# Last eight block halves in banks of their own, and a last norm with ScalarE's root

## The chip, the cores and the metric

One core of one Trainium2 chip runs the whole program. The metric is the device time of one execution in microseconds; less is better. The engines are TensorE (PE: matmuls, with their weight loads as PEld), VectorE (DVE), ScalarE (ACT), GpSimd (POOL) and SyncE (SP), which here only issues DMAs.

## The reference, cut to what matters

The program is one inference step of a hybrid decoder layer over 512 prompt positions and 8 sample tokens, with D = 1024. Only its end matters here: the down projection of the gated MLP, the residual add and the final norm.

```python
def rmsnorm(x, g):
    xf = x.astype(jnp.float32)
    y = xf * lax.rsqrt(jnp.mean(xf * xf, axis=-1, keepdims=True) + EPS)
    return y.astype(x.dtype) * g

# conv_ffn:       (jax.nn.silu(gate) * val) @ w_down      D_FF = 2816
# decoder_layer:  return h + y_ffn
# reference:      y_prompt = rmsnorm(hp, g_final); y_sample = rmsnorm(hs, g_final)
```

## The kernel before

Activations are kept transposed: `hT` is the residual as [128 channels, 8 blocks of channels, 2 halves of tokens, 260 tokens], so block d holds channels 128d to 128d+127, and a half holds 256 prompt positions and 4 sample tokens. A product in full precision is made of three reduced ones: the weight and the activation are each split in a high and a low part (`w_hi`, `w_lo`, `h_hi`, `h_lo`), and hi*hi, hi*lo and lo*hi are summed in PSUM. ScalarE makes the high parts, VectorE the low parts.

The down projection runs over three parts of the 22 hidden tiles (8, 8 and 6). The first two parts, and blocks 0 to 3 of the third, handle both halves of the tokens with one split weight (lines 1533 to 1553). The last four blocks of the third part (`D0` = 4 to 7) are done half by half (lines 1589 to 1617): first all four blocks for the first half, then, with the weights split once in `wl_hi` and `wl_lo`, all four for the second. Each of these eight block halves is 6 tiles times 3 products = 18 matmuls of 260 columns into PSUM; then VectorE adds the result to `hT` (line 1605, which the profile lists as the helper's line 120), ScalarE squares it (`sq`, line 1607), GpSimd adds the square to `acc4` (line 1609), and `final_block` lets ScalarE write `hT` times `g_final` to `hg`. PSUM has three tiles "pp" of two banks each and two tiles "t" of one bank. Here blocks 4 and 5 of a half share one "pp" tile, `ps[:, 0]` and `ps[:, 1]`, and so do blocks 6 and 7.

`half_norm` sums the squares over channels with matmuls against a column of ones (line 1567): 128, 128 and 4 tokens, one column of PSUM each. On the second half the last square isn't added by GpSimd but summed by a second set of those matmuls. VectorE scales the sums, adds eps and forms the reciprocal root by an integer first guess and three Newton steps (`rsqrt`, lines 216 to 228, 12 small operations). Two transposes and a small matmul spread the result over the partitions (lines 1577 and 1578), and ScalarE copies it to `R`. `half_store` then multiplies `hg` by `R` in three pieces of 3, 3 and 2 blocks, on VectorE, GpSimd and VectorE, and issues a store of each from SP, ScalarE and SP.

The order of the instructions on each engine is made by the framework's scheduler from the order of the program and the readiness of operands; `tc.high_priority()` moves the last norm up. A matmul that starts in a tile waits until the readers of the tile's former content are done. `half_norm(0)` and `half_store(0)` are called through the list `todo`, after block 4 of the second half.

Of the kernel before, what the change touches and what calls it, by code (L numbers as in the profile page):

```python
# [12 lines left out]
AF = mybir.ActivationFunctionType  # L13
OP = mybir.AluOpType
AX = mybir.AxisListType

P = 128
D = 1024
KT = D // P
SEQ = 512  # L20
NB = 8
HT = 260
# [12 lines left out]
EPS = 1e-6  # L35
# [66 lines left out]
def run(gen):  # L102
    for _ in gen:
        pass
# [3 lines left out]
def decoder_step(ctx: ExitStack, tc: tile.TileContext, A, O):  # L108
    nc = tc.nc
    dve, act, pe, pool, sp = nc.vector, nc.scalar, nc.tensor, nc.gpsimd, nc.sync  # L110
# [5 lines left out]
    def acopy(o, i, scale=1.0):  # L116
        act.activation(o, i, AF.Copy, scale=scale)  # L117

    def tt(o, a, b, op, eng=None):
        (eng or dve).tensor_tensor(o, a, b, op=op)  # L120
# [10 lines left out]
    def open_pool(name, side="left", psum=False):  # L131
        es = ExitStack()
        kw = {"space": bass.MemoryType.PSUM} if psum else {}
        p = es.enter_context(tc.tile_pool(name=name, bufs=1, reuse_waits="tile", side=side, **kw))
        return p, es

    def ptile(pool_, shape, tag, dt=F32, bufs=1, name=None):
        return pool_.tile(shape, dt, tag=tag, name=name or tag, bufs=bufs)
# [7 lines left out]
    rp, _e = open_pool("rp")  # L146
# [4 lines left out]
    ident = cst[:, C_ID:C_ID + 128]  # L151
    px0, es_px0 = open_pool("px0")
    hT = ptile(px0, [P, KT, 2, HT], "x0")
# [17 lines left out]
    ones = const.tile([P, 2], F32, name="ones")  # L171
# [4 lines left out]
    def load_w(src, kt=KT, name="w_raw"):  # L176

        t = ptile(wp, [P, KT, 256], "w_raw", bufs=2, name=name)
        sp.dma_start(t[:, :kt, :], src.rearrange("(k p) c -> p k c", p=P))
        return t  # L180
# [35 lines left out]
    def rsqrt(ms, n):  # L216
        i = ptile(rp, [P, 8], "rs_i", I32, bufs=2)[:, :n]
        y = ptile(rp, [P, 8], "rs_y", bufs=2)[:, :n]
        t = ptile(rp, [P, 8], "rs_t", bufs=2)[:, :n]
        hx = ptile(rp, [P, 8], "rs_hx", bufs=2)[:, :n]  # L220
        dve.tensor_scalar(i, ms.bitcast(I32), 1, None, op0=OP.logical_shift_right)
        dve.tensor_scalar(y.bitcast(I32), i, -1.0, float(0x5F3759DF), op0=OP.mult, op1=OP.add)
        dve.tensor_scalar(hx, ms, -0.5, None, op0=OP.mult)
        for _ in range(3):
            tt(t, y, y, OP.mult)
            tt(t, t, hx, OP.mult)
            dve.scalar_tensor_tensor(y, t, 1.5, y, op0=OP.add, op1=OP.mult)
        return y
# [59 lines left out]
    def bank(tag):  # L288
        p, n = ps_pool[tag]
        return ptile(p, [P, 2, 512] if tag.startswith("pp") else [P, 512], tag, bufs=n, name="ps_" + tag)  # L290
# [3 lines left out]
    def pp():  # L294
        return bank("pp")
# [901 lines left out]
    hT = ptile(hp, [P, KT, 2, HT], "hT")  # L1197
# [40 lines left out]
    for q in range(2):  # L1238
        raw = ptile(wp, [P, 4, 512], "w_raw", bufs=2, name="w_oa")
# [6 lines left out]
        for l in range(4):  # L1246
            d = 4 * q + l
            w = split_w(raw[:, :, l * P:(l + 1) * P], 4)
            ps = pp()
# [35 lines left out]
    raw = load_w(A["w_xq"][0][:, 0:256])  # L1285
# [133 lines left out]
    ff, _e = open_pool("ff")  # L1419
# [22 lines left out]
    for q in range(4):  # L1442
        raw = load_w(A["w_xo"][0][:, q * 256:(q + 1) * 256]) if q else None
        for l in range(2):
            d = 2 * q + l
            if q == 0:
                ps = ps_xo[l]
                project(ps, w_xo[l], xs_o, ks=range(6, KT))
            else:
                w = split_w(raw[:, :, l * P:(l + 1) * P])  # L1450
                ps = pp()
# [17 lines left out]
    w_down = A["w_down"][0]  # L1469
# [54 lines left out]
    parts = ((0, 8), (8, 16), (16, 22))  # L1524
# [3 lines left out]
    def final_block(d, hf=(0, 1)):  # L1528

        for r in hf:  # L1530
            acopy(hg[:, r, d], hT[:, d, r], scale=vec[:, 68 + d:69 + d])

    for pi, (j0, j1) in enumerate(parts):
# [5 lines left out]
        kt = j1 - j0  # L1539
        for q in range(4 if pi < 2 else 2):  # L1540
            raw = load_w(w_down[j0 * P:j1 * P, q * 256:(q + 1) * 256], kt)
            for l in range(2):
                d = 2 * q + l
                w = split_w(raw[:, :kt, l * P:(l + 1) * P], kt)
                ps = bank("pp")
                project(ps, w, lambda k: hid[j0 + k], 0, kt)
                tt(hT[:, d], hT[:, d], ps[:, :, :HT], OP.add)
                if pi == 2:
# [6 lines left out]
    D0 = 4  # L1555
    kt = parts[2][1] - parts[2][0]
    wl_hi, wl_lo = (ptile(ab3, [P, KT, 2, HT], t, F32R, name="wl").rearrange("p a r t -> p (a r t)")
                    [:, 0:(KT - D0) * kt * P].rearrange("p (d k c) -> p d k c", k=kt, c=P) for t in ("x3_hi", "x3_lo"))

    def half_norm(hf, *rest):  # L1560

        ps = bank("t")
        squares = (acc4[:, hf],) + rest
        for j, a in enumerate(squares):
            for i in range(3):
                n = P if i < 2 else 4
                pe.matmul(ps[0:n, i:i + 1], a[:, i * P:i * P + n], ones[:, 0:1], start=(j == 0 and i == 0),
                          stop=(j == len(squares) - 1), skip_group_check=True)
        ms = ptile(rp, [P, 8], "ss", bufs=2, name="ms")
        dve.memset(ms, 1.0)  # L1570
        with (tc.high_priority() if hf else ExitStack()):
            dve.tensor_scalar(ms[:, 0:2], ps[:, 0:2], 1.0 / D, EPS, op0=OP.mult, op1=OP.add)
            dve.tensor_scalar(ms[0:4, 2:3], ps[0:4, 2:3], 1.0 / D, EPS, op0=OP.mult, op1=OP.add)
            rs = rsqrt(ms[:, 0:3], 3)
            ps = bank("t")
            for i in range(2):
                pe.transpose(ps[:, i * P:(i + 1) * P], rs[:, i:i + 1].to_broadcast([P, P]), ident)
            pe.matmul(ps[:, 256:260], rs[0:4, 2:3].to_broadcast([4, P]), ident[0:4, 0:4], start=True, stop=True)
            R = ptile(rp, [P, 2, HT], "R", bufs=2, name="R4")[:, 0]
            acopy(R, ps[:, 0:HT])  # L1580
        return R

    def half_store(hf, R):
        for d0, d1, eng, q in ((0, 3, dve, sp), (5, 8, pool, act), (3, 5, dve, sp)):
            o = hg[:, hf, d0:d1]
            tt(o, o, R[:, None, :].to_broadcast([P, d1 - d0, HT]), OP.mult, eng)
            q.dma_start(O["y_t"][:, hf, d0:d1], o)

    todo = [lambda: final_block(D0 - 1)]
    for hf in range(2):  # L1590
        for d in range(D0, KT):
            dl, l = d - D0, d % 2
            if l == 0:
                ps = bank("pp")
                if hf == 0:
                    raw = load_w(w_down[parts[2][0] * P:, d * P:(d + 2) * P], kt)
            if hf == 0:
                with ExitStack():
                    acopy(wl_hi[:, dl], raw[:, :kt, l * P:(l + 1) * P])
                tt(wl_lo[:, dl], raw[:, :kt, l * P:(l + 1) * P], wl_hi[:, dl].bitcast(F32), OP.subtract)  # L1600
            for k in range(kt):
                xhi, xlo = hid[parts[2][0] + k]
                for j, (a, x) in enumerate(((wl_hi, xhi), (wl_hi, xlo), (wl_lo, xhi))):
                    pe.matmul(ps[:, l, :HT], a[:, dl, k, :], x[:, hf, :], start=(k + j == 0), stop=(k == kt - 1 and j == 2))  # L1604
            tt(hT[:, d, hf], hT[:, d, hf], ps[:, l, :HT], OP.add)
            sq = ptile(ff, [P, SEQ + NB], "sg", bufs=2, name="sqh")[:, 0:HT]
            act.activation(sq, hT[:, d, hf], AF.Square)
            if hf == 0 or d < KT - 1:
                pool.tensor_tensor(acc4[:, hf], acc4[:, hf], sq, op=OP.add)
            while todo:  # L1610
                todo.pop(0)()
            todo.append(lambda d=d, hf=hf: final_block(d, (hf,)))
        if hf == 0:
            todo.append(lambda: half_store(0, half_norm(0)))
    while todo:
        todo.pop(0)()
    half_store(1, half_norm(1, sq))


_OUTS = [("y_t", (P, 2, KT, HT)), ("kv_t", (6, P, 2, HT)), ("win_keep", (NB, WIN - 1, 2, 2, 64)),  # L1620
# [74 lines left out]
```

## Time and profile before

| | us |
|---|---|
| median of 3 runs | 899.33 (898.23 to 901.22) |
| the profiled execution, device time | 901.21 |
| its span, first to last instruction | 899.1 |
| TensorE matmuls busy | 857.2 (95%) |
| TensorE weight loads busy | 789.3 (88%) |
| VectorE, ScalarE, GpSimd busy | 567.5, 369.6, 121.6 |

Times in the rows are microseconds from the start of the span. Matmuls are pipelined: one of 260 columns shows about 0.28 us, and the next starts about 0.12 us after it. A row "x2" merges neighbours, and its time is that from the first start to the last end. In square brackets stands the idle time of the engine before the instruction, and what ended it. The granted clock of TensorE is 1.00 at 2.4 GHz and 0.50 at 1.2 GHz. VectorE's, ScalarE's and GpSimd's helper operations are listed under the helper's line (L120, L117).

### The profile page before, as it was taken

The numbers are of one execution on the slowest core, as the hardware profiler recorded it, in microseconds if no ns is written. First come the engines' busy times: TensorE is split into PE (matmuls) and PEld (weight loads), VectorE is DVE, ScalarE is ACT, GpSimd is POOL, SyncE is SP. The second block draws the span as 40 slices with busy tenths as digits, with TensorE's granted clock in tenths as the row PEclk, the third lists the DMA queues.
The fourth block names the chain that finished last, engine by engine and source line by source line (L and its number), as shares of the span: only waits on it lengthen the run. The fifth ranks groups of instructions, "written<-read, shape, count | busy, mean of one in ns | idle before, by whom it ended". The sixth has DMA issues, their size and how long they took to land.

```text
span 899.1 us, 17462 instructions
## 1 busy us (share of the span) xinstructions
PE 857.2 (95%) x7085; PEld 789.3 (88%) x7085; DVE 567.5 (63%) x1450; ACT 369.6 (41%) x684; POOL 121.6 (14%) x114
## 2 busy tenths in 40 slices
PE   7989999699999999999999999999999999999993
PEld 6978786587777789999889999999999999999993
DVE  6653173987665767788764578773377774367734
ACT  5432132566656546344343254441144442134541
POOL 6713033400000004000043000000000000000132
PEclk9988999979999999999999999999999999999995
DMA  8943795342332146477514643322333322332212
GB/s 281 322 153 107 269 354 199 117 154 97 106 118 71 47 132 213 143 236 250 179 47 118 230 137 98 94 93 83 87 84 85 90 94 94 95 94 84 81 36 95
DMA packets 108175, 122.84 MB, mean 137 GB/s; under 512 B 4592, under 2 KB 95088, under 8 KB 106032
## 3 DMA queue, kind: packets, MB, share of 16 engines
q1 hardware_dynamic: 103488, 100.79, 35.5%
q0 software_dynamic: 3600, 19.55, 5.9%
q10 hardware_dynamic: 1008, 1.40, 0.4%
q8 instruction: 55, 0.90, 0.4%
q14 instruction: 24, 0.20, 0.1%
HBM read 114.58 MB, written 10.69 MB: 139 GB/s over the span
## 4 chain that ended last, share of the span: by engine, by line
PE 85%; DVE 6%; DMA 4%; ACT 2%; issue 1%; SPq 0%; DVEq 0%; ACTq 0%; POOL 0%; POOLq 0%
PE ps_pp L204 56%; PE ps_tb L1132 3%; PE ps_sc L1002 3%; DMA w_u<-in_w_up_dram 3%; PE ps_o L1038 2%; PE ps_tb L1153 2%; PE ps_tb L973 2%; PE ps_tf L1031 2%; PE ps_pp L1604 2%; DVE w_lo L120 1%; PE ps_x L1322 1%; PE ps_x L1341 1%; ACT w_hi L117 1%; PE ps_s L1379 1%; DMA w_kv<-in_w_in_t_dram 1%
## 5 line engine op out<-in xcount | busy, mean ns | idle before, releaser
L204 PE MATMUL ps_pp<-x_hi,w_lo 128*128 128x260 f32 x832 | 169.2, 284 | 0.5 <-DVE w_lo L120 0.5
L204 PE MATMUL ps_pp<-x_hi,w_hi 128*128 128x260 f32 x832 | 169.5, 284 | 0.1
L204 PE MATMUL ps_pp<-x_lo,w_hi 128*128 128x260 f32 x832 | 167.8, 283 | 0.0
L204 PEld LDWEIGHTS ps_pp<-x_hi,w_lo 128*128 128x128 f32 x832 | 128.7, 188 | 1.2 <-DVE w_lo L120 0.7
L204 PEld LDWEIGHTS ps_pp<-x_hi,w_hi 128*128 128x128 f32 x832 | 128.7, 188 | 0.5 <-ACT w_hi L117 0.3
L204 PEld LDWEIGHTS ps_pp<-x_lo,w_hi 128*128 128x128 f32 x832 | 128.1, 188 | 0.4 <-issue 0.4
L117 ACT ACTIVATE w_hi<-w_raw 128x1024 fp32r<-128x1024 f32 (+1 forms) x52 | 54.2, 1043 | 107.6 <-PE ps_pp L204 85.9
L120 DVE TENSOR_TENSOR hT<-hT,ps_pp 128x520 f32<-128x520 f32 (+1 forms) x44 | 28.4, 646 | 88.6 <-PE ps_pp L204 74.5
L117 ACT ACTIVATE w_hi<-w_u 128x1024 fp32r<-128x1024 f32 x44 | 46.7, 1061 | 76.0 <-PE ps_pp L204 65.0
L120 DVE TENSOR_TENSOR w_lo<-w_raw,w_hi 128x1024 fp32r<-128x1024 f32 (+1 forms) x52 | 64.5, 1241 | 4.3 <-ACT w_hi L117 4.0
L204 PE MATMUL ps_pp<-h_lo,w_hi 128*128 128x260 f32 x304 | 61.3, 283 | 0.0
L204 PE MATMUL ps_pp<-h_hi,w_hi 128*128 128x260 f32 x304 | 61.2, 282 | 0.0
L204 PE MATMUL ps_pp<-h_hi,w_lo 128*128 128x260 f32 x304 | 61.1, 282 | 0.0
L120 DVE TENSOR_TENSOR ext<-ps_pp,R 128x512 f32<-128x512 f32 x44 | 30.4, 690 | 45.4 <-PE ps_pp L204 45.3
L120 DVE TENSOR_TENSOR w_lo<-w_u,w_hi 128x1024 fp32r<-128x1024 f32 x44 | 53.9, 1226 | 7.0 <-ACT w_hi L117 6.7
L204 PE MATMUL ps_pp<-xn_hi,w_hi 128*128 128x260 f32 x208 | 48.8, 316 | 5.0 <-ACT w_hi L117 2.9
L1551 POOL DMA_DIRECT2D out_ffn_t_dram<-last x1 | 0.6, 574 | 351.1 <-DVE last L114 351.1
L204 PE MATMUL ps_pp<-xn_lo,w_hi 128*128 128x260 f32 x208 | 46.5, 304 | 0.8 <-DVE xn_lo L129 0.7
L204 PEld LDWEIGHTS ps_pp<-h_hi,w_hi 128*128 128x128 f32 x304 | 46.9, 188 | 0.2 <-ACT h_hi L117 0.2
L204 PEld LDWEIGHTS ps_pp<-h_hi,w_lo 128*128 128x128 f32 x304 | 46.9, 188 | 0.0
L204 PEld LDWEIGHTS ps_pp<-h_lo,w_hi 128*128 128x128 f32 x304 | 46.8, 188 | 0.0
L204 PE MATMUL ps_pp<-xn_hi,w_lo 128*128 128x260 f32 x208 | 45.7, 302 | 0.3 <-DVE w_lo L120 0.3
(457 smaller groups left out, 1884.3 us busy)
## 6 DMA issues: line engine op xcount, KB each, us to landing
w_u<-in_w_up_dram SPq DMA_DIRECT2D x44, 512.0 KB, 4.6
xkr<-in_cache_mem_dram SPq DMA_DIRECT2D x16, 512.0 KB, 5.1
xvr<-in_cache_mem_dram SPq DMA_DIRECT2D x16, 512.0 KB, 6.2
w_raw<-in_w_down_dram SPq DMA_DIRECT2D x8, 1024.0 KB, 5.2
Kt<-in_k_t_dram SPq DMA_DIRECT2D x32, 128.0 KB, 4.0
w_raw<-in_w_in_t_dram SPq DMA_DIRECT2D x8, 512.0 KB, 4.3
w_raw<-in_w_xkv_dram SPq DMA_DIRECT2D x4, 1024.0 KB, 5.4
w_v<-in_w_xkv_dram SPq DMA_DIRECT2D x4, 1024.0 KB, 5.1
```

The source lines that it names most:

```text
L117: act.activation(o, i, AF.Copy, scale=scale)
L120: (eng or dve).tensor_tensor(o, a, b, op=op)
L204: pe.matmul(o, a[:, k, :], x[:, hf, :], start=(k == 0 and j == 0), stop=(k == kt - 1 and j == 2))
L973: pe.matmul(ps[:, :HT], a[:, k, :], y[x][:, k, hf, :], start=(k + j == 0), stop=(k == 3 and j == 2))
L1002: pe.matmul(ss_[hl][:, 0:c0 + nk], Qst[:, h, qc], k[:, g, u, 0:c0 + nk], start=(u == 0), stop=(u == 1))
L1031: pe.transpose(pt[:, hh * P:(hh + 1) * P], pr[hh][:, kb * P:(kb + 1) * P], ident)
L1038: pe.matmul(po[hp * 64:(hp + 1) * 64, g * 256:(g + 1) * 256], Vtok[:, br, kb - 1, g * 64:(g + 1) * 64], pTs[kb - 1][:, hp * 256:(hp + 1) * ...
L1132: pe.matmul(ps[:, 0:MEM], a[:, k, :], x[:, k, :], start=(k == 0 and j == 0), stop=(k == 7 and j == 2))
L1153: pe.matmul(ps[i], x[:, k, ts_], w[:, kl, :], start=(k == 0 and j == 0), stop=(k == KT - 1 and j == 2))
L1322: pe.matmul(s[:, ql * MEM:(ql + 1) * MEM], a[:, 2 * h + dh, hf, ql * P:(ql + 1) * P], x[:, 2 * h + dh, :], start=(n == 0), stop=(n == 5))
L1341: pe.matmul(po, v[:, mb, dh * P:(dh + 1) * P], x[:, mb, :], start=(mb + j == 0), stop=(mb + j == 3))
L1604: pe.matmul(ps[:, l, :HT], a[:, dl, k, :], x[:, hf, :], start=(k + j == 0), stop=(k == kt - 1 and j == 2))
```

## The change

Each of the last eight block halves takes a "pp" tile of its own and uses its first bank. The norm's third matmul takes the last 128 tokens of the half (132 to 259) instead of the last 4, and the third transpose likewise, so all columns have 128 rows. The root of the sum plus eps times D is taken on ScalarE; VectorE turns it into a reciprocal root with one Newton step, in four operations; the missing factor 2 sqrt(D) is put in the copy to `R`. A one-column root is taken after the first square. The last square of the first half, too, is summed by matmuls and not added by GpSimd. All of `hg` times `R` is done on VectorE in pieces of 3, 3 and 2 blocks, stored from SP, ScalarE and SP. For the first half these pieces are traced one per block of the second half.

```diff
+    eps_d = ptile(ff, [P, 1], "eps_d")
+    dve.memset(eps_d, EPS * D)
+    T3 = (0, P, HT - P)
+
     def half_norm(hf, *rest):
 
         ps = bank("t")
         squares = (acc4[:, hf],) + rest
         for j, a in enumerate(squares):
-            for i in range(3):
-                n = P if i < 2 else 4
-                pe.matmul(ps[0:n, i:i + 1], a[:, i * P:i * P + n], ones[:, 0:1], start=(j == 0 and i == 0),
-                          stop=(j == len(squares) - 1), skip_group_check=True)
-        ms = ptile(rp, [P, 8], "ss", bufs=2, name="ms")
-        dve.memset(ms, 1.0)
+            for i, t in enumerate(T3):
+                pe.matmul(ps[:, i:i + 1], a[:, t:t + P], ones[:, 0:1], start=(j + i == 0), stop=(j == len(squares) - 1),
+                          skip_group_check=True)
+        s = ptile(rp, [P, 8], "rs_y", bufs=2)[:, 0:3]
+        r = ptile(rp, [P, 8], "rs_t", bufs=2)[:, 0:3]
         with (tc.high_priority() if hf else ExitStack()):
-            dve.tensor_scalar(ms[:, 0:2], ps[:, 0:2], 1.0 / D, EPS, op0=OP.mult, op1=OP.add)
-            dve.tensor_scalar(ms[0:4, 2:3], ps[0:4, 2:3], 1.0 / D, EPS, op0=OP.mult, op1=OP.add)
-            rs = rsqrt(ms[:, 0:3], 3)
+
+            act.activation(s, ps[:, 0:3], AF.Sqrt, bias=eps_d)
+            dve.reciprocal(r, s)
+            dve.scalar_tensor_tensor(r, ps[:, 0:3], EPS * D, r, op0=OP.add, op1=OP.mult)
+            tt(s, s, r, OP.add)
+            dve.reciprocal(r, s)
             ps = bank("t")
-            for i in range(2):
-                pe.transpose(ps[:, i * P:(i + 1) * P], rs[:, i:i + 1].to_broadcast([P, P]), ident)
-            pe.matmul(ps[:, 256:260], rs[0:4, 2:3].to_broadcast([4, P]), ident[0:4, 0:4], start=True, stop=True)
+            for i, t in enumerate(T3):
+                pe.transpose(ps[:, t:t + P], r[:, i:i + 1].to_broadcast([P, P]), ident)
             R = ptile(rp, [P, 2, HT], "R", bufs=2, name="R4")[:, 0]
-            acopy(R, ps[:, 0:HT])
+            acopy(R, ps[:, 0:HT], scale=2.0 * float(D) ** 0.5)
         return R
 
     def half_store(hf, R):
-        for d0, d1, eng, q in ((0, 3, dve, sp), (5, 8, pool, act), (3, 5, dve, sp)):
+        for d0, d1, q in ((0, 3, sp), (3, 6, act), (6, 8, sp)):
             o = hg[:, hf, d0:d1]
-            tt(o, o, R[:, None, :].to_broadcast([P, d1 - d0, HT]), OP.mult, eng)
+            tt(o, o, R[:, None, :].to_broadcast([P, d1 - d0, HT]), OP.mult)
             q.dma_start(O["y_t"][:, hf, d0:d1], o)
+            yield
...
     for hf in range(2):
         for d in range(D0, KT):
             dl, l = d - D0, d % 2
...
-            if l == 0:
-                ps = bank("pp")
...
+            ps = bank("pp")[:, 0, :HT]
             for k in range(kt):
                 xhi, xlo = hid[parts[2][0] + k]
                 for j, (a, x) in enumerate(((wl_hi, xhi), (wl_hi, xlo), (wl_lo, xhi))):
-                    pe.matmul(ps[:, l, :HT], a[:, dl, k, :], x[:, hf, :], start=(k + j == 0), stop=(k == kt - 1 and j == 2))
-            tt(hT[:, d, hf], hT[:, d, hf], ps[:, l, :HT], OP.add)
+                    pe.matmul(ps, a[:, dl, k, :], x[:, hf, :], start=(k + j == 0), stop=(k == kt - 1 and j == 2))
+            tt(hT[:, d, hf], hT[:, d, hf], ps, OP.add)
             sq = ptile(ff, [P, SEQ + NB], "sg", bufs=2, name="sqh")[:, 0:HT]
             act.activation(sq, hT[:, d, hf], AF.Square)
-            if hf == 0 or d < KT - 1:
+            if hf == 0 and d == D0:
+                act.activation(ptile(rp, [P, 8], "rs_t", bufs=2)[:, 0:1], sq[:, 0:1], AF.Sqrt)
+            if d < KT - 1:
                 pool.tensor_tensor(acc4[:, hf], acc4[:, hf], sq, op=OP.add)
             while todo:
                 todo.pop(0)()
             todo.append(lambda d=d, hf=hf: final_block(d, (hf,)))
+            if hf == 1:
+                if d == D0:
+                    stores = half_store(0, half_norm(0, sq0))
+                next(stores, None)
+        sq0 = sq
         if hf == 0:
-            todo.append(lambda: half_store(0, half_norm(0)))
+            todo.pop()()
+    run(stores)
     while todo:
         todo.pop(0)()
-    half_store(1, half_norm(1, sq))
+    run(half_store(1, half_norm(1, sq)))
```

## Rows read from the trace of the kernel before

**Rows 1.** Chain of waits, last 24 us: start, duration, engine, tile, line.

```profile
880.69 4.28 PE ps_pp L1604 x18
...
885.00 0.44 DVE hT L120
...
885.99 1.15 PE ps_t L1567 x6
...
887.16 0.16 DVE ms L1572
...
889.69 0.66 PE ps_t L1577 x2
...
890.90 0.40 ACT R L117
...
891.32 0.97 DVE hg L120
```

**Rows 2.** List of waits, 860 to 899.2: us in total, times, longest.

```profile
PE ps_pp L1604 <- DVE hT L120: 2.8, 1, 2.8
```

**Rows 3.** Stage windows: PE, PEld, DVE, ACT, POOL busy; PEclk; DMA share; GB/s.

```profile
877.00:879.90 2.90, 0.85 (x8) 0.64 (x6) 2.90 (x2) 0.66 (x2) 2.74 (x2) 1.00 0.24 96
...
880.70:885.00 4.30, 4.30 (x20) 4.30 (x21) 0.01 (x1) 0.82 (x2) 0.74 (x1) 0.50 0.29 110
```

**Rows 4.** Timeline of VectorE and GpSimd: start, duration, instruction, idle before.

```profile
862.34 0.42 DVE L120 TENSOR_TENSOR hT<-hT,ps_pp 128x260 f32<-128x260 f32 x1 [0.98 <-PE ps_pp L1604]
...
865.28 0.43 DVE L120 TENSOR_TENSOR hT<-hT,ps_pp 128x260 f32<-128x260 f32 x1 [2.52 <-PE ps_pp L1604]
...
866.85 0.42 DVE L120 TENSOR_TENSOR hT<-hT,ps_pp 128x260 f32<-128x260 f32 x1 [1.15 <-PE ps_pp L1604]
...
876.47 1.86 POOL L120 TENSOR_TENSOR hg<-hg,R 128x780 f32<-128x780 f32 x1 [3.29 <-ACT R L117]
876.66 3.64 DVE L120 TENSOR_TENSOR hg<-hg,R 128x780 f32<-128x780 f32 x2
```

**Rows 5.** Timeline of TensorE, first norm's sums and an earlier norm's, 498 to 506.

```profile
859.97 0.28 PE L1604 MATMUL ps_pp<-h_hi,wl 128*128 128x260 f32 x1
...
871.74 0.73 PE L1567 MATMUL ps_t<-ones,acc 128*128 128x1 f32 x6 [0.35 <-POOL acc L1609]
...
498.35 0.28 PE L255 MATMUL ps_t<-ones,acc 128*128 128x1 f32 x2
...
499.83 0.36 PE L255 MATMUL ps_t<-ones,sq 128*128 128x1 f32 x2
...
506.10 0.60 PE L233 MATMUL ps_t<-cst,rs_y 128*128 128x128 f32 x4
```

**Rows 6.** Timeline from 890 on: the last products and stores.

```profile
891.32 3.21 DVE L120 TENSOR_TENSOR hg<-hg,R 128x780 f32<-128x780 f32 x2 [1.78 <-ACT R L117]
891.36 2.61 POOL L120 TENSOR_TENSOR hg<-hg,R 128x780 f32<-128x780 f32 x1 [9.34 <-ACT R L117]
892.32 2.61 SPq L1587 DMA_DIRECT2D out_y_t_dram<-hg  x2
894.00 0.35 ACTq L1587 DMA_DIRECT2D out_y_t_dram<-hg  x1
```

**Rows 7.** Groups of ScalarE and VectorE, whole span: busy us, mean ns, idle before.

```profile
L173 ACT ACT_TABLE_LOAD x1 | 1.3, 1283 | 2.2 <-issue 2.2
L1504 ACT ACT_TABLE_LOAD x1 | 1.3, 1283 | 0.0
...
L1367 ACT ACTIVATE xs<-xs,xmx_s 128x16 f32<-128x16 f32 x4 | 1.2, 295 | 0.0
...
L1061 DVE RECIPROCAL s<-s 128x8 f32<-128x8 f32 x4 | 0.8, 198 | 0.0
```

**Rows 8.** Timeline of TensorE, 45 to 56, around a fall of the clock.

```profile
49.58 0.80 PE L204 MATMUL ps_pp<-xn_hi,w_hi 128*128 128x260 f32 x2 [2.07 <-ACT w_hi L117]
...
53.99 0.40 PE L204 MATMUL ps_pp<-xn_hi,w_hi 128*128 128x260 f32 x2
```

More of the change, by code (lines that the diff above doesn't have):

```diff
@@ L1585, in half_store @@
             o = hg[:, hf, d0:d1]
-            tt(o, o, R[:, None, :].to_broadcast([P, d1 - d0, HT]), OP.mult, eng)
+            tt(o, o, R[:, None, :].to_broadcast([P, d1 - d0, HT]), OP.mult)
             q.dma_start(O["y_t"][:, hf, d0:d1], o)
+            yield
     todo = [lambda: final_block(D0 - 1)]
+    stores = iter(())
     for hf in range(2):
@@ L1592, in decoder_step @@
             dl, l = d - D0, d % 2
-            if l == 0:
-                ps = bank("pp")
-                if hf == 0:
-                    raw = load_w(w_down[parts[2][0] * P:, d * P:(d + 2) * P], kt)
+            if l == 0 and hf == 0:
+                raw = load_w(w_down[parts[2][0] * P:, d * P:(d + 2) * P], kt)
             if hf == 0:
-                with ExitStack():
-                    acopy(wl_hi[:, dl], raw[:, :kt, l * P:(l + 1) * P])
+                acopy(wl_hi[:, dl], raw[:, :kt, l * P:(l + 1) * P])
                 tt(wl_lo[:, dl], raw[:, :kt, l * P:(l + 1) * P], wl_hi[:, dl].bitcast(F32), OP.subtract)
+            ps = bank("pp")[:, 0, :HT]
             for k in range(kt):
```

## The prediction, made before the changed kernel had run

> **What bounds the kernel now.** I began with the page: TensorE is busy 857.2 us of a span of 899.1, and its busy tenths are nines from the middle on, except for the very last slice. So the body is bound by matmuls, the diff leaves every one of them as it is, and only the last 40 us can change. The chain of waits in order of time [rows 1] shows what ends last there: behind the two VectorE multiplications of `half_store(0)` come the 18 matmuls of the very last block half (d=7, second half), its add, the squares' sums, a run of small VectorE operations, the transposes, the copy of R, the multiplication of the result. The list of waits [rows 2] names the one long wait on TensorE: 2.8 us, on the VectorE add of `hT`. The stage table [rows 3] shows the clock: 1.00 granted while TensorE stood idle in most of 877.0 to 879.9, then 0.50, the lower level of 1.2 GHz, for all of the last half.
>
> Two things produce that wait. First, d=6 and d=7 share one tile `ps`, and a matmul into one half of it waits for the add that reads the other half. The adds show it [rows 4]: the streams are equally long, but the adds of d=4, 5, 6 come at 862.34, 865.28, 866.85, so 2.94 and 1.57 apart. The second of each pair is held back, and six matmuls of the next pair (about 0.72 us) are run first as filler. The last pair has no next one. Second, the add it waits for stands on VectorE behind `half_store(0)`: there one 780-column and one 520-column product take 3.64 us together, while GpSimd multiplies its own 780 columns [rows 4]. Alone a 780-column product takes 0.97 us [rows 1], so two would be 1.6.
>
> **The change, part by part**, against the profiled execution (901.21 us, span 899.1).
>
> (a) Own bank pairs. Each half takes its own `bank("pp")` of three, so a half waits only for the add three halves earlier. For d=7 of the second pass that is d=4 of the same pass, over long before; no wait is left. I rebuild TensorE's stream from 859.97 [rows 5]. Eight halves cost 8 x 18 x 0.1205 = 17.35 us at the full clock (the pitch is 859.97 to the first add at 862.34, less 0.2 of latency, over 18). The sums of the first norm become 12 full matmuls instead of 6. The 16 sums of the earlier norm run from 498.35 to 500.19 at full clock, 0.11 each [rows 5], so 1.33 us. Three transposes: four took 0.60 [rows 5], so about 0.50. The adds of d=4 and d=6 are 4.51 apart [rows 4] where 36 pitches make 4.34, so a pair slips by 0.17; four pairs make 0.68, of which I keep half, 0.35, since the pair's own wait goes. End: 859.97 + 17.35 + 1.33 + 0.50 + 0.35 + 0.2 latency = 879.7. The old stall before the sums, where TensorE waited for GpSimd's `acc` (871.74 row, [rows 5]), goes, because the last square is now summed by TensorE directly. The add of d=7 thus starts at 879.7 instead of 885.00: **-5.3 us**. About 3.0 of it is the wait, 2.1 the clock (4.28 against 2.17 for 18 matmuls), the rest the 0.5 stall, less the added sums. Bounds: if the transposes of the first norm stand early in TensorE's order and their chain is late by half a microsecond, and a 0.6 us piece is on VectorE when the last add is due, -4.2; if no slip is left, -5.6.
>
> (b) What (a) is covered by. VectorE gets all the products of the first half: 0.97 + 0.97 + 0.65 = 2.6 us in three pieces, spread over three iterations, with no GpSimd product beside them. Adds behind a piece are late by up to 0.97 us, and nobody but ScalarE's square and GpSimd's sum waits for them. The store of the second piece is issued on ScalarE; it waits there for VectorE's product, and queued behind it are squares and copies of later blocks. SP holds only stores here. If R came 1 us late, that would cost the square of d=6, not yet TensorE. Taken at nothing; its open cost is in the bound -4.2.
>
> (c) The last norm's sums: 6 full columns instead of 4 full and 2 narrow. The old six took 1.15 us at 0.50 [rows 1, 3]. TensorE's waits ahead of them are now the add and the square alone, about 1.0 us, which is less than the 2.8 us before the fall, so I take the full clock: 5 x 0.11 + 0.25 = 0.80, **-0.35**. At the low clock, with twice the pitch, 5 x 0.22 + 0.35 = 1.45, so +0.3.
>
> (d) Square root. Old: 887.16 to the transposes at 889.69, so 2.53 us of fourteen small VectorE operations [rows 1]. New: one ScalarE root of 3 columns with a bias tile, nearest to the 16-column activation with a tile operand, 0.295 [rows 7]; four dependent VectorE operations at the old chain's pitch of 0.195, reciprocals among them (0.198 for 8 columns, [rows 7]), 0.80; hops 0.15. Together 1.25, **-1.25**. No row shows a root; between 0.25 and 0.8 for it and its hops the bounds are -1.5 and -0.9.
>
> The root needs another table. The trace has exactly two table loads, 1.283 us each [rows 7]. The change puts a one-column root behind the square of d=4 in the first pass, so a third load of 1.28 lands near 863, where ScalarE has gaps of 2 us between squares and nothing of TensorE waits for it: cost nothing. Uncovered, on the last norm, it costs 1.28.
>
> The Trainium skill ("ScalarE: Activation LUTs", What ACT_TABLE_LOAD costs) prices a switch at about 2.66 us, a drain of 1.38 included. The row shows 1.283 and no idle time before it, so the trace does not bear the drain out here. By the page's figure an uncovered load would make (d) a loss of 1.4 instead of about nothing; as covered, neither moves the sum.
>
> (e) Transposes: 889.69 to R's copy at 890.90 was 1.21 at the low clock [rows 1]. Three transposes replace two and a two-pass product. I take the low clock here still (TensorE waits a second time, 1.25 us, with little work between): two took 0.66 at the low clock, a third adds 0.22, so 0.88 and a hop instead of 1.21, **-0.3**; at the full clock -0.7.
>
> (f) The last products. Old: 0.97, then the second VectorE piece ends at 894.53, because GpSimd's 2.61 us product [rows 6] lies beside it. New: 0.97 + 0.97 + 0.65 = 2.6 plus hops, so the third store is issued about 0.6 us earlier than the old last one, and ScalarE's some 0.7 earlier [rows 6]. Five of the eight blocks must still pass after the first store, so I take **-0.45** (-0.6 to -0.3). From the last issue's end (894.93) to the end of the span, 4.2 us, stays.
>
> Sum: -5.3 - 0.35 - 1.25 - 0.3 - 0.45 = **-7.65**; the bounds add up to -8.75 and -5.4. The profiled execution would become 893.6. Against the median of 899.33 (the profiled one was 1.9 above it) the forecast is **891.7**.
>
> **The rivals.**
> 1. The preloaded table doesn't last: a square or copy between the preload and the last root puts it out. Then a load of 1.28 stands in the last norm, and another before the first norm's transposes, where TensorE would wait part of it: 891.7 + 1.3 to 2.6 = 893.0 to 894.3. Against it: squares, copies and scalings ran under both tables of the trace without a third load [rows 7].
> 2. The change doesn't do what it says: the last half still waits for VectorE, through the pair or the order of instructions. The wait would then be the latency of an add and one piece, some 0.6 to 1.6 us instead of 3.0, for GpSimd is gone from it, and too short for the clock to fall: 892.3 to 893.3. Against it: the held-back adds show that the pair is what ties them [rows 4].
> 3. Slower than before: tables alternate. If square and copy had no place in the root's table, two loads would stand in the first norm (before the root, before R's copy) and two in the last: 4 x 1.283 = 5.1 us. In the first norm TensorE would stand at its transposes for 2.6 us. Waits of 2.07 and 2.8 us were followed by the low clock [rows 2, 8], which after the former held for 4.3 us of matmuls (49.58 to 53.9, [rows 8]), some 20 matmuls at 0.096 extra, 1.9 us; held for all 54 that are left (the last half of before never got it back), 5.2. Together 5.1 + 5.2 + 0.35 against 7.65: 899.33 + 3.0 = 902.3; with the quick recovery, 899.0. It decides where the stall is as long as those two waits and the low clock stays to the end. The evidence against rival 1 speaks against it too.
>
> For rival 3 the Trainium skill (same page, Table sets: the hidden batching unit) says that cheap functions such as copy and identity are in every set, which is against it; square is not in that sentence's list, and its drain would price four switches at 10.6 us, an estimate from the page.
>
> **How the numbers follow.** A change under 0.3%, 2.7 us, can't be told from none. Forecast 891.7: 0.75. Rival 1: 0.09. Rival 2: 0.08. Rival 3: 0.05, of which 0.02 is slower by over 0.3% and 0.03 within. Another 0.03 is for an unforeseen order of instructions that eats most of the gain, within 0.3%. So faster 0.92, same 0.06, slower 0.02. The range takes the best sum (-8.75, 890.6) less one for the spread of the shown runs (898.23 to 901.22), and the other way the worst sum (-5.4, 893.9) with rival 1's first load on it (1.28): 889.6 to 895.2.
>
> **What would show it.** In the new trace: no wait of TensorE over 0.5 us between 860 and the last of 144 stream matmuls, which end near 879.7; clock 1.00 through it; 18 matmuls of the last half in 2.2 us; one table load near 863 and none behind it; about 1.25 us from the last sum to the transposes; no GpSimd product of `hg`, and three products of 0.97, 0.97 and 0.65 on VectorE. A second load after 863, or a TensorE wait over 2 us at the first norm's transposes, would make it wrong.

## The result, and the profile after

| | before | after |
|---|---|---|
| median | 899.33 us (898.23 to 901.22) | 891.65 us (890.19 to 893.21) |
| ratio, with its 95% interval | | 0.9912 (0.9893 to 0.9932) |
| span of the profiled execution | 899.1 us | 889.9 us |
| of it, from the first of the 144 matmuls to the end ("the tail") | 39.13 us | 30.33 us |

The change makes the kernel 7.7 us faster, 6.1 to 9.6 by the interval; 891.7 had been forecast. The tail fell by 8.80 us, so of the 9.2 us between the two spans 0.4 stem from the program ahead of it, which the diff doesn't touch.

The list of waits of the changed kernel, 850 to 890, holds no `ps_pp` row of L1609, where [rows 2] has 2.8 us. What TensorE still waits for (us in total, times, longest):

```profile
PE ps_t L1583 <- DVE rs_t L1580: 1.7, 2, 1.3
...
PE ps_t L1570 <- POOL acc L1616: 0.3, 1, 0.3
```

The stage windows of the changed kernel (busy of PE, PEld, DVE, ACT, POOL; PEclk; DMA share; GB/s). The first is the stream up to the last half, then come the last half, the sums, TensorE's wait for the root, the transposes:

```profile
859.60:877.00 17.40, 17.00 (x143) 16.79 (x142) 7.19 (x15) 8.20 (x19) 4.83 (x6) 1.00 0.04 17
877.00:879.40 2.40, 2.33 (x20) 2.12 (x18) 1.21 (x3) 0.82 (x2) 0.85 (x2) 1.00 0.83 321
879.60:881.20 1.60, 1.56 (x12) 1.47 (x12) 0.19 (x1) 0.82 (x2) 0.00 (x0) 1.00 0.04 10
881.20:882.50 1.30, 0.00 (x0) 0.01 (x1) 0.68 (x4) 0.26 (x1) 0.00 (x0) 0.95 0.00 0
882.50:883.40 0.90, 0.87 (x3) 0.49 (x3) 0.00 (x0) 0.00 (x0) 0.00 (x0) 0.50 0.00 0
```

Against [rows 3]: the last half runs at a granted clock of 1.00 in 2.3 us, where it took 4.3 at 0.50. Only the last three transposes see the low clock.

The chain of waits of the changed kernel, in order of time (start, duration, engine, tile, line), which answers to [rows 1]:

```profile
875.80 2.04 DVE hg L120 x2
...
878.27 0.43 ACT sqh L1612
...
878.81 0.78 POOLq L1704
...
879.63 1.57 PE ps_t L1570 x12
...
881.23 0.27 ACT rs_y L1576
...
882.52 0.89 PE ps_t L1583 x3
...
883.43 0.40 ACT R L117
...
883.85 0.97 DVE hg L120
```

The last half is no longer in it: VectorE's products lead over the add of d=6, its square on ScalarE and GpSimd's add to the sums. From the root at 881.23 to the transposes there are now 1.29 us, where [rows 1] has 2.53 (887.16 to 889.69). Then the timeline of ScalarE and VectorE in the changed kernel: the table load, the last add, the last products.

```profile
863.29 1.28 ACT L1614 ACT_TABLE_LOAD   x1
864.58 0.20 ACT L1614 ACTIVATE rs_t<-sqh 128x1 f32<-128x1 f32 x1
...
879.37 0.43 DVE L120 TENSOR_TENSOR hT<-hT,ps_pp 128x260 f32<-128x260 f32 x1 [1.19 <-PE ps_pp L1609]
...
883.85 2.46 DVE L120 TENSOR_TENSOR hg<-hg,R 128x780 f32<-128x780 f32 x3 [1.48 <-ACT R L117]
```

The load stands where it was forecast, "near 863", and it is the only one besides the two of [rows 7]. The three products take 2.46 us, against 3.21 for two beside GpSimd's in [rows 6]. To the end of the span there are 6.05 us from the first product (883.85 to 889.9) where there were 7.78 (891.32 to 899.1), which the forecast had not seen coming.

### The profile page after: what moved, and what is told of

Same layout as the page of the kernel before. It is cut to its first block, busy times and chain, and to the rows that moved or that the text cites. A ratio compares the mean times of both kernels' runs of the same rounds, so it can differ in the third digit from the quotient of the medians.

```text
span 889.9 us, 17455 instructions
## 1 busy us (share of the span) xinstructions
PE 853.3 (96%) x7089; PEld 785.4 (88%) x7089; DVE 564.2 (63%) x1431; ACT 371.2 (42%) x688; POOL 115.7 (13%) x111
## 4 chain that ended last, share of the span: by engine, by line
PE 85%; DVE 6%; DMA 4%; ACT 2%; issue 1%; SPq 0%; DVEq 0%; POOLq 0%; ACTq 0%
PE ps_pp L204 57%; PE ps_sc L1002 3%; PE ps_tb L1132 3%; DMA w_u<-in_w_up_dram 3%; PE ps_o L1038 3%; PE ps_tb L1153 2%; PE ps_tb L973 2%; PE ps_tf L1031 2%; DVE w_lo L120 1%; PE ps_x L1341 1%; PE ps_x L1322 1%; PE ps_pp L1609 1%; PE ps_s L1379 1%; DMA Wk<-in_win_k_t_dram 1%; PE ps_tb L759 1%
```

## The experiments

They ran on other chips, where the kernel before takes medians of 934.67 to 937.46 us. The ratios have intervals of about 0.3% to either side, 2.8 us, so they can't tell most variants from each other. The tail can, because it is the same to 0.06 us when the changed kernel is profiled on two chips; what it can vary by, in otherwise equal profiles, is 0.36 us that hang on the clock of the last transposes (both below). I cut it in three at points that every trace shows: A, from the first of the 144 matmuls to the first operation on the last norm's sums (`ms` at L1572, or the root); B, from there to the first product of the result; C, from there to the end of the span. Every line is one profiled execution. The kernel before has its profile on the first chip only, but its B and C come back within 0.08 us in the variants that keep its norm or its products.

| kernel | ratio (95%) | A | B | C | tail |
|---|---|---|---|---|---|
| before | 1 | 27.19 | 4.16 | 7.78 | 39.13 |
| after | 0.9912 (0.9893 to 0.9932) | 21.66 | 2.62 | 6.05 | 30.33 |
| after, other chip | 0.9914 (0.9883 to 0.9946) | 21.66 | 2.63 | 5.98 | 30.27 |
| before + own pairs | 0.9969 (0.9941 to 0.9997) | 22.29 | 4.15 | 7.73 | 34.17 |
| before + VectorE products | 0.9947 (0.9922 to 0.9973) | 23.69 | 4.15 | 6.09 | 33.93 |
| before + root | 0.9956 (0.9928 to 0.9984) | 23.59 | 2.27 | 7.77 | 33.63 |
| after, shared pairs | 0.9913 (0.9886 to 0.9941) | 22.87 | 2.62 | 5.98 | 31.47 |
| after, GpSimd product | 0.9932 (0.9901 to 0.9964) | 21.78 | 2.27 | 7.72 | 31.77 |
| after, old norm | 0.9921 (0.9895 to 0.9947) | 21.40 | 4.17 | 5.98 | 31.55 |
| before + 24 matmuls | 0.9980 (0.9954 to 1.0005) | 24.96 | 4.16 | 7.70 | 36.82 |
| after, no early root | 0.9902 (0.9873 to 0.9932) | 21.43 | 2.27 | 6.08 | 29.78 |
| after, four pieces | 0.9914 (0.9884 to 0.9945) | 21.66 | 2.63 | 5.99 | 30.28 |
| after, five transposes | 0.9914 (0.9882 to 0.9946) | 21.63 | 2.60 | 5.93 | 30.16 |
| after, late GpSimd add | 0.9970 (0.9944 to 0.9996) | 21.66 | 2.26 | 8.41 | 32.33 |

**Each of the three parts alone.** First the own bank pairs, put into the kernel before:

```diff
+            ps = bank("pp")[:, 0, :HT]
-            if l == 0:
-                ps = bank("pp")
```

> The kernel before with one part of the change: each of the last eight block halves in a bank pair of its own. Theory (the shared pair makes TensorE wait for the add of d=6, and VectorE's products beside GpSimd's only make that add late): TensorE runs the last half without a wait at the full clock, but the last add still stands behind VectorE's 3.6 us of products, so it starts some 20.7 us after the first of the 144 matmuls (25.0 before, 19.8 with the whole change); about 3.5 us faster, 895.8. Rival (GpSimd beside VectorE is the whole cause and the pair doesn't matter): a wait of 2 to 3 us and the low clock stay, 898.3 to 899.3.

Then the products of both halves on VectorE, traced one per block of the second half:

```diff
-        for d0, d1, eng, q in ((0, 3, dve, sp), (5, 8, pool, act), (3, 5, dve, sp)):
+        for d0, d1, q in ((0, 3, sp), (3, 6, act), (6, 8, sp)):
+            yield
+                if d == D0:
+                    stores = half_store(0, half_norm(0))
+                next(stores, None)
```

> The kernel before with one part of the change: all products of the result on VectorE in three pieces, those of the first half spread over the blocks of the second. Pairs stay shared, the root stays on VectorE. Theory: the add of d=6 is late by at most one or two pieces, so TensorE waits about 1 us before the last half instead of 2.8, too short for the clock to fall; the last add starts some 21 us after the first matmul; with 0.6 us of the last products about 4.5 us faster, 894.8. Rival (the pair alone makes the wait and the low clock): the wait stays near 3 us, only the last products gain, 898.3. Rival (GpSimd alone): no wait at all, 893.4.

And the norm with ScalarE's root, sums, transposes and early root as in the change, with shared pairs and GpSimd's product as before:

```diff
+            act.activation(s, ps[:, 0:3], AF.Sqrt, bias=eps_d)
+            dve.reciprocal(r, s)
+            dve.scalar_tensor_tensor(r, ps[:, 0:3], EPS * D, r, op0=OP.add, op1=OP.mult)
+            tt(s, s, r, OP.add)
+            dve.reciprocal(r, s)
-            rs = rsqrt(ms[:, 0:3], 3)
```

> The kernel before with one part of the change: the norm by ScalarE's root with a Newton step and full columns; pairs shared, GpSimd multiplies a piece. Theory: the last norm gives 1.25 and the transposes 0.3; the first norm is done 1.2 us sooner, so VectorE's products and the add behind them are too, and TensorE waits 1.8 us instead of 3.0; if the clock then stays at 1.00, another 2.1: 4.9 us faster, 894.5, otherwise 2.8 faster, 896.5. Rival (only the end of the chain counts, additive): 1.55 faster, 897.8.

The pairs alone shorten the tail by 4.96 us, the products alone by 5.20, the root alone by 5.50, each somewhat more than was expected (3.5, 4.5, 4.9). That is 15.7 together, and all three at once bring 8.80. B and C add up: B falls by 1.9 with the root alone and by 1.5 in the whole (the difference is the clock of the last transposes, below), C by 1.7 with VectorE's products alone and in the whole. What doesn't add up is A: 4.90, 3.50 and 3.60 alone, 5.53 in the whole. Where A came from is in the waits of TensorE. Products alone, list of waits:

```profile
PE ps_pp L1606 <- DVE hT L120: 1.6, 1, 1.6
```

Root alone, list of waits:

```profile
PE ps_pp L1609 <- DVE hT L120: 1.4, 1, 1.4
```

Own pairs alone, list of waits; here there is no `ps_pp` row, but the sums now wait for GpSimd's last `acc`:

```profile
PE ps_t L1567 <- POOL acc L1609: 1.7, 1, 1.7
```

That `acc` takes in the square of d=6, whose add VectorE starts only behind its own products beside GpSimd's. Timeline of VectorE, the products and the last two adds:

```profile
912.66 3.26 DVE L120 TENSOR_TENSOR hg<-hg,R 128x780 f32<-128x780 f32 x2 [1.25 <-ACT R L117]
915.84 0.74 DVE L120 TENSOR_TENSOR hT<-hT,ps_pp 128x260 f32<-128x260 f32 x2
```

So the same block of products holds up the end here too, over the square and GpSimd's add instead of over the pair. The last add itself came 19.35 us behind the start of the stream, where 20.7 had been expected.

With the products alone and with the root alone the pair is still shared, and the wait is there, but of about half the length: without GpSimd's product beside it VectorE's block of products is shorter, and with the root R is ready earlier, so the block starts earlier. Behind 1.6 and 1.4 us the granted clock was still 1.00. The last half of the kernel with the root alone, in its chain of waits (the time from the first start to the last end), is 2.43 us; [rows 1] has 4.28:

```profile
917.85 2.43 PE ps_pp L1609 x18
```

So any one of the three gets the clock of the last half back, 1.85 us by these two rows, and at least 1.2 us of wait, and only the first to come is paid for them. By the medians alone the overlap isn't proved: the three ratios fall short of 1 by 0.31, 0.53 and 0.44%, 1.28 together with an interval of about 0.5 to either side, against 0.86 to 0.88 for the whole.

**Each of the three parts taken out of the whole.** Pairs shared again:

```diff
-            ps = bank("pp")[:, 0, :HT]
+            if l == 0:
+                ps = bank("pp")
```

> The changed kernel with the pairs shared again. The tail is counted from the first of the last 144 matmuls to the end of the span: 39.1 us before, 30.3 with the change, 33.6 to 34.2 with one part alone. Theory (the three parts each shorten the same wait, so each is worth little when the other two are there): TensorE waits about 1 us for the add of d=6, the clock stays, the tail is 31.4. Rival (the pair is worth the 5.3 us that the prediction gave it): the tail is 35 or more.

The last half waits again, for the add of d=6 behind one 0.70 us piece. Timeline of TensorE, first matmul of the last half:

```profile
914.67 0.39 PE L1610 MATMUL ps_pp<-h_hi,wl 128*128 128x260 f32 x1 [0.53 <-DVE hT L120]
```

A is 1.21 us longer, the clock stays. The pairs are thus worth 1.2 us as the last of the three parts and 4.9 as the first.

GpSimd's product back in place:

```diff
-        for d0, d1, q in ((0, 3, sp), (3, 6, act), (6, 8, sp)):
+        for d0, d1, eng, q in ((0, 3, dve, sp), (5, 8, pool, act), (3, 5, dve, sp)):
```

> The changed kernel with the third part alone undone: half_store again gives GpSimd blocks 5 to 7 of the products and VectorE 3 and 2 blocks, stored from SP, ScalarE and SP as before; own bank pairs and the root stay. The tail counts from the first of the 144 matmuls to the end of the span (changed kernel 30.33 us). Theory, from the kernels run so far: the products of the first half cost the stream nothing here, since with own pairs no matmul waits for VectorE (last add 19.6 to 20.0 after the start of the stream), and the whole price lies behind the last norm, where first product to end of span was 7.7 to 7.8 with GpSimd's product in four kernels and 6.0 to 6.1 without it in four: 1.7 us, tail 32.0. Rival 1, as my prediction sized this part: 0.45 us, tail 30.8. Rival 2: VectorE's add of the last block comes late behind the slowed products of the first half, as before the change: a wait on hT of 1 us or more, tail 33 or over.

A is longer by 0.12 us only: with own pairs no matmul of the stream waits for VectorE's slow block (the last add is 19.80 us behind the start, as in the changed kernel), and the sums wait 0.48 us for GpSimd's add instead of 0.30. C is 7.72 instead of 5.98, so the theory of 1.7 holds and the 0.45 of my prediction doesn't. (The tail grew by 1.50, not 1.7, because the transposes happened to run at full clock: B 2.27.)

The norm with VectorE's integer guess and three steps again (the diff of the root turned round, sums and transposes too):

> The changed kernel with the norm as before: integer first guess and three Newton steps on VectorE, and 4 columns of the last tokens instead of 128. Own pairs and VectorE's products stay. Theory: the last chain is 1.25 us longer and the transposes 0.3, the sums 0.1 shorter; the first half's products come 1.2 us later and hold the last adds up to 0.6; no wait on TensorE, tail 31.7 to 32.4. Rival (the root also carries part of the wait that own pairs should have removed): 34 or more.

B is 4.17 instead of 2.63. A is 0.26 shorter: the old sums are narrower, and TensorE doesn't wait ahead of the first norm's transposes, where the changed kernel has 0.40 us; what each gives wasn't separated. Net 1.28.

**The clock.** Is it the idle time that loses the clock? In the kernel before, 24 needless matmuls, whose result nobody reads, stand between the halves of d=6 and d=7:

```diff
+            if hf == 1 and d == KT - 1:
+                fill = bank("t")[:, 0:HT]
+                for i in range(24):
+                    pe.matmul(fill, wl_hi[:, 0, 0, :], hid[parts[2][0]][0][:, 0, :], start=True, stop=True)
```

> The kernel before with 24 needless matmuls of 260 columns put between d=6 and d=7 of the second pass, into a bank of their own; their result isn't used. They take 2.9 us, the length of the wait. Theory (the idle time makes the clock fall): the granted clock stays 1.00 through the last half, whose 18 matmuls take 2.2 instead of 4.3 us, and the sums 0.7 instead of 1.15; the tail is 39.1 - 2.1 - 0.4 = 36.6, though more matmuls run. Rival (the clock falls at this place whatever TensorE does): 4.3 us again, tail 39.1.

Stage windows of that kernel, the needless matmuls and the last half (columns as above):

```profile
911.30:914.30 3.00, 3.00 (x26) 2.83 (x24) 2.98 (x3) 0.00 (x0) 2.09 (x2) 1.00 0.50 192
914.30:916.70 2.40, 2.40 (x21) 2.36 (x21) 0.00 (x0) 0.82 (x2) 0.75 (x1) 1.00 0.55 210
```

The wait is filled with 3.0 us of work, which is longer than the wait was, and A is 2.23 us shorter: the last half and the sums run at 1.00. The gain in the tail is 2.31 us; in the ratio (0.9980) it isn't beyond its interval. So the low clock of [rows 3] belonged to the idle 2.8 us.

The same was tried on the last transposes, with five needless transposes of the root in the wait ahead of them (and the last products in four pieces, of which below):

```diff
+            if hf:
+                idle = bank("pp")[:, 0, 0:P]
+                for _ in range(5):
+                    pe.transpose(idle, s[:, 0:1].to_broadcast([P, P]), ident)
```

> The changed kernel with the last half's products in pieces of 1, 2, 3 and 2 blocks and, between the last norm's sums and its transposes, five transposes of ScalarE's root into an idle bank, whose result nobody reads. Their question is the clock: in the changed kernel TensorE waits 1.33 us ahead of the last three transposes and these take 0.87 us, at a granted clock of 0.50. Theory: idle time is what loses the clock, so with the wait shortened to under 0.9 us by needless work the three transposes take 0.53 us and the tail is 0.35 us shorter, 29.9 us against 30.3. Rival: the clock falls all the same, or the needless transposes are still running when the reciprocal root is ready; then nothing is gained or up to 0.3 us is lost (30.3 to 30.6).

Timeline of TensorE in that kernel, the needless and the needed ones:

```profile
917.39 0.76 PE L1580 MATMUL ps_pp<-cst,rs_y 128*128 128x128 f32 x5 [0.35 <-ACT rs_y L1576]
918.71 0.51 PE L1587 MATMUL ps_t<-cst,rs_t 128*128 128x128 f32 x3 [0.56 <-DVE rs_t L1584]
```

The needed ones take 0.51 us, as the theory said. That it was the needless ones that kept the clock isn't shown by it: one of the rows below has 0.51 without them too. And VectorE's add overwrites what the needless ones read and waited 0.37 us for them, so B fell by 0.03 us only and nothing was gained.

How firm the clock is behind a wait of this length is shown by the changed kernel unaltered on another chip:

> The changed kernel unaltered, on the same chip as its variants, so that their tails can be set beside its own. If the tail belongs to the kernel and not to the chip it is 30.3 us within 0.4, as on the chip of the first measurement, and the ratio to the kernel before is that 30.3 us against 39.1 gives: some 8 to 9 us of about 937, 0.990 to 0.9915. If the chip matters, the wait or the clock around the last transposes differs from the first profile.

A, B and C are there again within 0.07 us, the wait of 1.33 us and the 0.88 us of transposes too:

```profile
918.69 0.88 PE L1583 MATMUL ps_t<-cst,rs_t 128*128 128x128 f32 x3 [1.33 <-DVE rs_t L1580]
```

In the kernel with a late GpSimd add (below), which is the same up to here, the same wait is followed by the full clock:

```profile
915.12 0.51 PE L1583 MATMUL ps_t<-cst,rs_t 128*128 128x128 f32 x3 [1.33 <-DVE rs_t L1580]
```

Behind this wait of 1.33 or 1.34 us the transposes took 0.87 or 0.88 us in four profiles and 0.51 in four. What decides stays open. For the 1.4 and 1.6 us above it means that the full clock behind them is seen in one execution each, and may not be in every one.

**The table load.** The early root left out of the changed kernel:

```diff
-            if hf == 0 and d == D0:
-                act.activation(ptile(rp, [P, 8], "rs_t", bufs=2)[:, 0:1], sq[:, 0:1], AF.Sqrt)
```

> The changed kernel without the one-column root that loads the table early. Theory of the prediction as rival 1 priced it: the load of 1.28 stands in the first norm before its root, TensorE stands at the transposes up to 1.3 us longer, 892.9. Rival: the load needs no operand and runs in ScalarE's 2.04 us gap before the first norm's root, so nothing changes, 891.7.

Timeline of ScalarE around the first norm's root:

```profile
905.92 0.50 ACT L117 ACTIVATE hg<-hT,vec 128x260 f32<-128x260 f32 x1
906.44 1.28 ACT L1576 ACT_TABLE_LOAD   x1
908.47 0.26 ACT L1576 ACTIVATE rs_y<-ps_t,eps_d 128x3 f32<-128x3 f32 x1 [0.74 <-PE ps_t L1570]
```

The load doesn't wait for the operand of its root. It ran while the sums were still being made, and 0.74 us of idle time follow it. Nothing is lost; the early root does no work in this kernel. That the tail is 0.5 us shorter than the changed kernel's goes, for 0.36 of it, to transposes that ran at full clock, and it can't be told from nothing in the ratio. The Trainium skill ("ScalarE: Activation LUTs", What ACT_TABLE_LOAD costs) adds a drain of about 1.38 us to a load; neither here nor at 863.29 in the changed kernel, where the next activation starts 1.29 us after the load did, does a row show one.

**The last stores.** Finer first pieces, 1, 2, 3 and 2 blocks for the second half:

```diff
-        for d0, d1, q in ((0, 3, sp), (3, 6, act), (6, 8, sp)):
+        for d0, d1, q in (((0, 3, sp), (3, 6, act), (6, 8, sp)), ((0, 1, sp), (1, 3, act), (3, 6, sp), (6, 8, act)))[hf]:
```

> The changed kernel with the last half's products in pieces of 1, 2, 3 and 2 blocks, stored from SP, ScalarE, SP, ScalarE, instead of 3, 3, 2. Theory (the end is bound by 2.7 us of store data that can't start before the first piece): data start 0.55 us sooner and run without a gap, the tail is 29.8. Rival (the last piece's time on VectorE and its issue bound the end): one more product and issue, nothing won or 0.2 lost, 30.3 to 30.5.

C is 5.99, as with three pieces, and the tail 30.28, as the rival had it: the data start earlier, flow with gaps and end at the same time.

That leaves the 1.7 us of C. Up to the end of the store data only 0.7 of it is found: narrow windows show data up to 5.4 us behind the first product in the kernel before, and up to 4.7 in the changed kernel. The rest, some 1.0 us, lies behind the data, between instructions that the kernel's text doesn't hold: those of the end of the program (L1691 in the kernel before, L1704 after). The listing of that line in the kernel before (count; durations in ns, least, median and most; first and last start in us):

```profile
L1691 POOLq EVENT_SEMAPHORE  x4: 17/17/17, 898.3 to 899.0; - x4
L1691 POOLq DRAIN  x3: 46/103/6907, 891.3 to 898.8; - x3
L1691 SPq DRAIN  x3: 7/7/7, 897.2 to 898.5; - x3
```

The same in the changed kernel:

```profile
L1704 POOLq EVENT_SEMAPHORE  x4: 17/17/17, 889.1 to 889.8; - x4
L1704 POOLq DRAIN  x3: 46/103/5023, 878.8 to 889.6; - x3
L1704 SPq DRAIN  x3: 7/7/7, 889.0 to 889.3; - x3
```

SyncE's first drain stands 0.5 us behind the last store data in both, at 897.2 and 889.0, so 5.9 and 5.2 us behind the first product. From it to the end of the span it is 1.9 and 0.9 us: here lies the other 1.0.

The longest drain of GpSimd's queue begins with its last operation: 6.91 us with the 2.61 us product, 5.02 with a 0.74 us add. Both times it ends some 4.3 us behind the operation. Before, that is 891.3 + 6.9 = 898.2, and the rest of the closing begins at 898.3; after, it is over at 883.8, long before the stores. Is that the cause? One needless add of GpSimd behind the last product of the changed kernel, whose sum nobody reads:

```diff
     run(half_store(1, half_norm(1, sq)))
+    pool.tensor_tensor(acc4[:, 1], acc4[:, 1], hg[:, 1, KT - 1], op=OP.add)
```

> The changed kernel with one needless GpSimd addition of 260 columns behind the last product of the result (its sum goes to acc4 and is used nowhere); stores, VectorE's products and everything ahead of them are as in the changed kernel. It measures by itself what a late GpSimd instruction costs at the end of the program. In all kernels that end with GpSimd's 2.61 us product, GpSimd's closing drain is listed with 6.91 us from the start of that product, so 4.3 us behind its end, and the span ends 0.9 us later; where GpSimd's last work is a 0.74 us add, the drain lasts 5.02, again 4.3 behind its end, and is over long before the stores. Theory: this drain, and not the stores, closed the kernel before. The needless add starts some 2.5 us after the first product, ends at 3.25, its drain at 7.5, and the span 0.85 later: first product to end of span 8.3 to 8.4 instead of 5.98 to 6.05, tail 32.6. Rival: the end goes by the landing of the stores and the drain is beside the point: 6.0, tail 30.3.

Timeline of GpSimd in that kernel:

```profile
918.73 0.73 POOL L1631 TENSOR_TENSOR acc<-acc,hg 128x260 f32<-128x260 f32 x1 [6.55 <-DVE hg L120]
```

Listing of its closing line:

```profile
L1705 POOLq EVENT_SEMAPHORE  x4: 17/17/17, 923.8 to 924.4; - x4
L1705 POOLq DRAIN  x3: 46/103/5017, 918.7 to 924.2; - x3
L1705 SPq DRAIN  x3: 7/7/7, 921.3 to 924.0; - x3
```

The add ends at 919.46, its drain at 918.7 + 5.0 = 923.7, the span at 924.5. C is 8.41, the 8.3 to 8.4 of the theory, and the stores are done as early as without it: SyncE's first drain stands at 921.3, 5.2 us behind the first product. An addition of 0.73 us, of use to no one, costs 2.4 us at the end of the program. So it was GpSimd's drain that closed the kernel before, and in the changed one it is the stores.

## Why the prediction was right, and where it wasn't

The forecast was 891.7, the median is 891.65. That they agree so closely is luck: the tail of the profile fell by 8.80 us where the terms add up to 7.65, just beyond the best bound of 8.75, and the medians differ by 7.68 with an interval of 1.8 to either side. By term:

| term | forecast | measured in the whole |
|---|---|---|
| (a) last add, from the start of the stream | -5.3 | -5.23 (25.03 to 19.80) |
| (c) last add to root | -0.35 | -0.30 (2.16 to 1.86) |
| (d) to the transposes | -1.25 | -1.24 (2.53 to 1.29) |
| (e) transposes to R's copy | -0.3 | -0.30 (1.21 to 0.91) |
| (f) first product, and from it to the end | -0.45 | -1.73 (7.78 to 6.05) |

- **(a)**: the size and the place are right. No wait of TensorE in the stream is longer than 0.40 us, and that is at the first norm's transposes. The clock is 1.00, and the rebuilt stream of 19.7 us was 19.80. The clock's share was put a little too high at 2.1, since the 4.28 us run to the end of the last matmul and the 2.17 set against them don't: with the 24 needless matmuls 1.83 us are gained ahead of the last add (25.03 to 23.20).
- **What was wrong in (a) is to whom it was credited.** The prediction named two causes of the wait, the shared pair and VectorE's block, and then put all 5.3 to the pair and took the products in (b), and the earlier R in (d), at nothing for the stream. Alone, each of these moves A by 3.5 and 3.6 us; the pair does 4.9 as the first and 1.2 as the last. Rival 2 came close, for it said what a wait left over would be once GpSimd is gone from it: 0.6 to 1.6 us and no low clock. With pairs shared it was 0.5 of wait and 1.2 of A, clock 1.00. For the sum it made no difference, since all three parts came together.
- **(b)**: right. The add of d=6 stands behind a product until 877.77, some 0.6 us late, and no matmul of the stream waits for it. Through its square and GpSimd's add it holds up the sums by 0.30 us, which costs nothing: the last square's sums come 0.99 us behind the last add, and 0.99 too with shared pairs, where no wait for `acc` is listed.
- **(c)**: right: the six new sums stand in a window of granted clock 1.00, as was taken.
- **(d)**: right, and the root is 0.26 us, where the nearest row gave 0.295. The cover that was named, an early load, wasn't needed: the load moves ahead by itself. Rivals 1 and 3 fell with the load list, one load near 863 and none behind it.
- **(e)**: right for the profiled execution. At full clock, as in four of the variants, it would have been -0.66.
- **(f)**: wrong. The step that failed is the sentence that the 4.2 us from the last issue's end to the end of the span "stays". It went to 3.18 (886.72 to 889.9). I took the closing for a fixed distance behind the last store. In the kernel before, it was GpSimd's drain, 4.3 us behind GpSimd's own product, and the change removed that product. The part that I did cost, the stores issued earlier, is worth 0.7 by the data, not 0.45.

## What to carry to other kernels

When a long wait has several causes, cost each part of a change as the first and as the last one made; here the same part was worth 4.9 or 1.2 us. At the end of a program look at what each engine's queue does behind its last operation, and keep late work off GpSimd: an add of 0.73 us cost 2.4. Cost a wait of TensorE with the clock behind it, and look whether a shorter wait would already keep the clock.

## What the runs showed of the hardware

- GpSimd's closing drain ended 4.3 us behind its last operation in every kernel profiled here, whether that was a product of 2.61 us or an add of 0.74.
- A table load of ScalarE ran 2.03 us ahead of the root that needed it, in idle time, while the root still waited.
- Beside GpSimd a small VectorE operation cost four times its price. The timeline of VectorE and GpSimd in the changed kernel, first norm:

```profile
872.47 0.74 POOL L1616 TENSOR_TENSOR acc<-acc,sqh 128x260 f32<-128x260 f32 x1 [4.35 <-ACT sqh L1612]
...
872.60 0.63 DVE L120 TENSOR_TENSOR rs_y<-rs_y,rs_t 128x3 f32<-128x3 f32 x1
```

  VectorE's add of three columns ends 0.02 us behind GpSimd's add; in the last norm, with GpSimd idle, the same operation takes 0.16. The Trainium skill ("SBUF — State Buffer", SBUF: two separate sides) has the two engines share a pair of ports to the on-chip memory as a lock that is held for the whole instruction, and names a VectorE operation with two inputs from there beside a GpSimd one that reads there; these rows agree, and so does the kernel with GpSimd's product put back, where VectorE's 520-column product beside it ends at 924.09, 0.56 us behind GpSimd's at 923.53.
- A wait of 1.33 us ahead of the last transposes was followed by the granted clock 0.50 in some executions and 1.00 in others, of the same instructions; 2.56 us, with the old norm, by 0.66 us for two transposes, the time of [rows 1], in every one of the five kernels that have it.
